# A new order of loads and steps at the start of a two-layer backbone kernel

## The chip, the cores and the metric

The kernel runs on one core of one Trainium2 chip. The core has the engines PE (matrix products, with its weight loads shown apart as PEld), DVE (vector), ACT (scalar functions), POOL (general) and SP (here it only issues transfers). Each engine takes its own instructions in order and waits on semaphores for the others. The metric is the device time in microseconds of one execution.

## The reference, cut to what matters

The model has two layers over 256 latent tokens `x` and 256 context tokens `h` of width 1024. The first sub-layer is a SwiGLU of both token sets, each normalised and modulated with its own scale and shift:

```
m  = silu(c) @ ada_w[0] + ada_b[0];   mc = silu(c_ctx) @ ada_w[0] + ada_b[0]
u  = rmsnorm(x, norm_g[0, 0]) * (1 + m[1]) + m[0]       # the same for h with mc
x += 0.5 * m[2] * ((silu(u @ wg) * (u @ wu)) @ wd)      # wg, wu: 1024 x 2816; wd: 2816 x 1024
```

Then come a state-space mixer, a second SwiGLU, and a second layer with a pooling mixer between two SwiGLUs, each sub-layer with its own scale, shift and gate out of `ada_w`. Only the start of the first sub-layer is changed.

## The kernel before

Activations lie with channels on the partitions: eight tiles of 128 channels by 512 tokens (256 of context, 256 latent). A weight block of 128 output channels is one load of 128x1024 floats (512 KB). Each product of float32 values is made of three matmuls on parts rounded to fp32r: ACT rounds the weight (`hi`, L203), DVE takes the rest (`lo`, L208), the operand is split likewise (`uh`, `ul`), and `mm3` (L216 to L218) adds high x high, low x high, high x low.

The start of the kernel, called the stage below, makes the operands of the first products and the first six weight blocks' products. It is written as a string, `WAVE`: each letter is one step, and the n-th occurrence of a letter is the step's n-th index. The order of the letters is the order in which the instructions are handed to the framework, which fixes each engine's queue at build time and may let an instruction that it holds ready pass earlier ones that wait.

- `X` loads one block of 128 tokens as two halves of 512 channels (tokens on the partitions), `v` (DVE) and `q` (ACT) square and sum the halves, `z` (DVE) adds the two sums, `r` (POOL) takes the power -0.5, and `s` (DVE, eight of them) scales a half by it.
- `A` loads two tiles of the scale and shift weights for one block of 128 channels (`adan`, ten buffers), `c` multiplies them with silu(c) on PE (two groups of instructions, one for each tile), `R` copies the row out (ACT), `e` turns it into columns on PE, `f` adds the constants (DVE).
- `t` turns the scaled tokens of one channel block on PE into the one bank `xc`, `m` scales and shifts out of that bank (DVE), `u` rounds (ACT), `n` takes the rest (DVE). Then one of eight operands is there.
- `L` loads a weight block (six, in six buffers), `h` rounds it (ACT), `k` takes the rest (DVE).
- `b` and `B` spread silu(c) over the partitions for later use.
- `p` is one cell: the product of one weight block with one operand, three matmuls of 512 columns. There are 6 x 8 cells, and the string `CELLS` gives their order ("21" is block 2 with operand 1).

Behind the stage the products of the other weight blocks follow, of two blocks and 16 cells for each index `f`. ACT's `sg` (L336) takes the first block of a pair when its eight cells are done. Among these products the weights for the other scales, shifts and gates are loaded and multiplied on DVE (`adaw`, L142 and L145); their buffers take the place of those of `adan`, so their loads wait for the stage's last `m`.

Of the kernel before, what the change touches and what calls it, by code (L numbers as in the profile page):

```python
# [15 lines left out]
P = 128  # L16
# [29 lines left out]

WAVE = (
    "AAXXXXLbAbBAcBALcRvqAezbRrfAqvebLBfzqvrqvzBzrshsrscALLLsktRcmeRefutfchnmpRckuetRenphfpf"  # L50
    "cmcRkuethpnpfhpmphkpRpukeppnpfpskppspspsptpmputpmpnutpmpnutpmpnuppnpppppppppppppppppppp"
)
CELLS = "00 10 01 11 20 02 12 21 22 30 31 32 03 13 23 33 40 41 42 43 50 51 52 04 14 05 15 24 06 07 16 17 25 26 27 34 35 36 37 44 45 46 47 53 54 55 56 57"

POOL_O = (1, 3)
POOL_Z = (1, 3)
# [10 lines left out]
def tile_hybrid_backbone(  # L67
# [20 lines left out]
    v, sc, pe, gp = nc.vector, nc.scalar, nc.tensor, nc.gpsimd  # L88
# [13 lines left out]
    def bank(nm, tag):  # L102
        if tag == "c":
            turn[0] ^= 1
            tag = f"c{turn[0]}"
        return ps.tile([P, 512], F32, tag=f"ps{tag}", name=nm, bufs=PSUM_BANKS[tag])

    def tmp(nm, tag, n=512):
        return tp.tile([P, 512], F32, tag=f"t{tag}", name=nm)[:, 0:n]
# [12 lines left out]
    XH = [xres.tile([P, 2 * S], F32, name=f"x{d}") for d in range(KD)]  # L122
    X = [t[:, LAT] for t in XH]
    cs = const.tile([P, 4 * P], F32, name="cs")
    ident, tri = cs[:, 0:P], [cs[:, P : 2 * P], cs[:, 2 * P : 3 * P]]
# [49 lines left out]
    def scale_cols(l, i, sub, nm):  # L175

        s = mcol(l, i, 3 * sub + 1, nm + "s")
        o = const.tile([P, KD], F32, name=nm + "a")
        g0 = C_NG + (3 * l + sub) * KD
        v.scalar_tensor_tensor(o, s, 1.0, pk[:, g0 : g0 + KD], op0=ALU.add, op1=ALU.mult)  # L180
        return o
# [100 lines left out]
    def utiles(T):  # L282
        uh = [upool[0].tile([P, T], F32R, name=f"uh{d}", tag=f"uh{d}") for d in range(KD)]
        ul = [upool[0].tile([P, T], F32R, name=f"ul{d}", tag=f"ul{d}") for d in range(KD)]
        return uh, ul
# [92 lines left out]
    u = utiles(2 * S)  # L378
    with ExitStack() as st:
# [22 lines left out]
        ads, prs, xcs, mts, raws, his, ws, outs = [], [], [], [], [], [], [], {}  # L402
# [31 lines left out]
        def w_b(j):  # L434
# [3 lines left out]
                pe.transpose(o[:, i * P : (i + 1) * P], cT[:, k % KD, k // KD : k // KD + 1].to_broadcast([P, P]), ident)  # L438
            bcs.append(o)

        def w_B(j):
            sc.activation(cb2[j // 2][:, (j % 2) * 512 : (j % 2 + 1) * 512], bcs[j], AF.Copy)

# [33 lines left out]
            )  # L477
            v.tensor_scalar(b00[:, d, :], pr[:, 2:4], col(C_AB, d), None, op0=ALU.add)

        def w_t(d):  # L480

            assert at["s"] >= 4 + d // 4 * 4
            x = bank("xc", "c1")
            for j in range(4):
                c = slice(d % 4 * P, (d % 4 + 1) * P)
                pe.transpose(x[:, j * P : (j + 1) * P], XH[2 * j + d // 4][:, c], ident)
            xcs.append(x)

        def w_m(d):
            assert len(xcs) > d and at["f"] > d  # L490
            x = xcs[d]
            t = tmp("mt", "a")
            for tok, i in ((ONE, 1), (LAT, 0)):
                a, b = a00[:, d, i : i + 1], b00[:, d, i : i + 1]
                v.tensor_scalar(t[:, tok], x[:, tok], a, b, op0=ALU.mult, op1=ALU.add)
            mts.append(t)
# [16 lines left out]
        def w_p(i):  # L513
            b, k = (int(c) for c in CELLS.split()[i])
            assert at["k"] > b and at["n"] > k
            if k == 0:
                outs[b] = bank("gu", "a" if b < 4 else "b")
            prod(outs[b], ws[b], k, u, ALL)

        steps = {  # L520
            "X": w_X, "v": w_v, "q": w_q, "z": w_z, "r": w_r, "s": w_s, "b": w_b, "B": w_B, "A": w_A, "c": w_c, "R": w_R,
            "e": w_e, "f": w_f, "t": w_t, "m": w_m, "u": w_u, "n": w_n, "L": w_L, "h": w_h, "k": w_k, "p": w_p,
        }
        at = dict.fromkeys(steps, 0)
        for what in WAVE:
            steps[what](at[what])
            at[what] += 1
        assert sorted(CELLS.split()) == [f"{b}{k}" for b in range(6) for k in range(KD)]
        assert [at[i] for i in "bBXvqzrsAcReftmunLhkp"] == [4, 4] + [4] * 5 + [8] * 10 + [6] * 3 + [48]
        st2.close()  # L530
        later = deque((XH[d], hxT[d * P : (d + 1) * P, :]) for d in range(KD))
        later.append((cs[:, P : 3 * P], tris))
# [57 lines left out]
    with ExitStack() as st:  # L590
# [4 lines left out]
        u = utiles(2 * S)  # L595
        a = [vecs[0].a, scale_cols(0, 1, 1, "a011")]
        b = [vecs[0].b, mcol(0, 1, 3, "b011")]
# [266 lines left out]
        o = ready.pop(24)  # L864
# [7 lines left out]
        def t64(nm, tag):  # L872
            return tmp(nm, tag, 256).rearrange("p (j c) -> p j c", c=64)

        dtk = scp.tile([P, 4, 64], F32, name="dtk")
        e, w, nr, ln = t64("dte", "a"), t64("dtw", "a"), t64("dtn", "b"), t64("dtl", "b")
# [29 lines left out]
        for d in range(2):  # L906
            c = slice(32 * d, 32 * d + 32)
# [17 lines left out]
        for j, d, k in ((0, 0, 1), (1, 1, 0)):  # L925
            c = slice(32 * d, 32 * d + 32)
# [4 lines left out]
        for d in range(2):  # L931
            c = slice(32 * d, 32 * d + 32)
# [14 lines left out]
        at = dict.fromkeys(steps, 0)  # L947
# [113 lines left out]
    for g in range(NG):  # L1061
        o = bank("pq", "b")[:, 0:S]
        channels(o, g, lambda t, k: t[k][:, S : S + 1].to_broadcast([P, P]))
        t = XH[g][:, ONE]
# [10 lines left out]
    for g in range(NG):  # L1075
        qh, ql = [], []
        for j in range(2):
            q = tmp("q", "b", S)
            v.scalar_tensor_tensor(q, pq[g, j], rtok[:, j : j + 1], bq[g], op0=ALU.mult, op1=ALU.add)
            a = work.tile([P, S], F32R, tag="qh", name="qh", bufs=3)  # L1080
            sc.activation(a, q, AF.Copy)
            b = work.tile([P, S], F32R, tag="ql", name="ql", bufs=3)
# [3 lines left out]
        for dd in range(2):  # L1086
            d = 2 * g + dd
            o = bank("pp", "c")[:, 0:S]
            pmh, pml = pm[g // 2]
            for j in range(2):  # L1090
                c = slice((2 * (g % 2) + j) * S, (2 * (g % 2) + j + 1) * S)
                dc = slice(dd * P, (dd + 1) * P)
                mm3(o, qh[j][:, dc], ql[j][:, dc], pmh[:, c], pml[:, c], j == 0, j == 1)
            t = tmp("pt", "d", S)
# [8 lines left out]
    for d2 in range(KD // 2):  # L1103
        o = tp.tile([P, 2, S], F32, tag="t" + "abcd"[d2], name="ot")
        for q in range(2):
            d = 2 * d2 + q
# [4 lines left out]
def _layout(inputs):  # L1111
    import numpy as np

    a = {k: np.asarray(x) for k, x in inputs.items()}
    f = np.float32

    def cols(x):
        return x.reshape(-1, P).T

    def tiles(w, nk):  # L1120

        n = w.shape[1] // P
        return w.reshape(nk, P, n, P).transpose(2, 1, 0, 3).reshape(n, P, nk * P)

    pack = np.concatenate(
        [
            cols(a["norm_g"]), cols(a["final_g"]), cols(a["ada_b"]),
            a["ssd_conv_w"][0].reshape(5, 24, P).transpose(2, 1, 0).reshape(P, 120),
            cols(a["ssd_conv_b"]), cols(a["pool_b"]), cols(a["pool_scale"]),
            np.concatenate([np.zeros(64, f), a["ssd_dt_bias"].reshape(64)])[:, None],  # L1130
            np.broadcast_to(a["ssd_a_log"].reshape(1, 64), (P, 64)),
            np.broadcast_to(a["ssd_d"].reshape(1, 32), (P, 32)),
            np.stack([a["c"].reshape(D), a["c_ctx"].reshape(D)]).reshape(2, KD, P).transpose(2, 1, 0).reshape(P, 16),
        ],
        axis=1,
    )
    assert pack.shape[1] == C_END
    i = np.arange(P)
    tris = np.concatenate(
        [i[:, None] <= i[None, :], i[:, None] >= i[None, :]], axis=1  # L1140
    ).astype(f)
    pm = np.zeros((NG, S, S))
    rows, width = S // 64, 64
    for g, w in enumerate((2, 4, 8, 16)):
        def box(n):
            p = np.arange(n)
            hi, lo = np.minimum(p + w - w // 2, n), np.maximum(p - w // 2, 0)
            return ((p[None, :] >= lo[:, None]) & (p[None, :] < hi[:, None])) / (hi - lo)[:, None]

        pm[g] = np.kron(box(rows), box(width)) - np.eye(S)  # L1150

    pmat = pm.transpose(0, 2, 1).reshape(2, 2, 2, P, S).transpose(0, 3, 1, 2, 4).reshape(2, P, 4 * S).astype(f)
    w_in = a["ssd_w_in"][0]
    wgu = np.stack(
        [
            np.stack([np.stack([tiles(a[n][l, s], KD) for n in ("ffn_w_gate", "ffn_w_up")]) for s in range(2)])
            for l in range(2)
        ]
    )
    wd = np.stack([np.stack([tiles(a["ffn_w_down"][l, s], NF) for s in range(2)]) for l in range(2)])  # L1160
    win = np.concatenate([tiles(w_in[:, 2048:5120], KD), tiles(w_in[:, 5056:5184], KD)])
    wz = w_in[:, :2048].reshape(4, 2, P, 4, 512).transpose(3, 0, 2, 1, 4).reshape(4, 4, P, 1024)
    wout = a["ssd_w_out"][0].reshape(4, 4, P, 4, 2, P).transpose(0, 3, 2, 4, 1, 5).reshape(4, 4, P, 1024)
    pw = a["pool_w"][0].reshape(2, 2, 2, P, 256).transpose(0, 3, 1, 2, 4).reshape(2, P, 1024)

    adan = np.stack([tiles(a["ada_w"][0][:, i * D : (i + 1) * D], KD).reshape(KD, P, KD, P) for i in (1, 0)], axis=3)
    adan = adan.reshape(KD, P, 2 * D)
    ada = np.stack([a["ada_w"][l].T.reshape(72, P, D) for l in range(2)])
    return {
        "hx": np.concatenate([a["ctx"][0], a["x"][0]]),  # L1170
        "hxT": np.concatenate([a["ctx"][0].T, a["x"][0].T], axis=1),
                "pack": pack, "idn": np.eye(P, dtype=f), "tris": tris, "pmat": pmat, "gnorm": a["ssd_norm_g"].reshape(1, 2048),
        "ada": ada, "adan": adan, "wgu": wgu, "wd": wd, "win": win, "wz": wz,
        "wout": wout, "poolw": pw,
    }
# [20 lines left out]
```

## Time and profile before

| | |
|---|---|
| timed runs | 1315.9 us median of 3 (1314.4 to 1316.13) |
| the profiled execution | 1308.84 us, of which the span of all instructions 1307.1 us |
| busy share of the span | PE 95%, PEld 85%, DVE 74%, ACT 46%, POOL 12% |
| first of 40 slices (0 to 32.7 us) | PE 50%, DVE 30%, granted clock of PE 0.7, transfers 90% or more |
| the slices after it | PE mostly 90% or more |
| mean granted clock of PE | 0.984 |

An engine's busy time counts its instructions, without semaphore waits and without issuing transfers. Matmuls are pipelined, so the length of one is longer than its distance to the next. The granted clock is given as a part of 2.4 GHz.

### The profile page before, as it was taken

Reading aid. Unit: us, or ns where it says so; the run is one execution under the profiler, and the core shown is the slowest. Engines: PE = TensorE matmul, PEld = TensorE weight load, DVE = VectorE, ACT = ScalarE, POOL = GpSimd, SP = SyncE. Lnnn points to the kernel's source line nnn. Section 1 sums busy time; section 2 is a strip of 40 time slices with the busy share of each in tenths; the row PEclk is TensorE's granted clock in tenths of the full one; section 3 lists DMA queues with packets and bytes.
Section 4 is the critical chain, followed back from the end, with each engine's and each line's share of the span. In section 5 each row is a group of like instructions: output and inputs, shape, how many; then the busy total and the mean of one; then the engine's idle time right before and its main releaser. Section 6 shows DMA issues by size and latency. Waiting matters only on the chain.

```text
span 1307.1 us, 21106 instructions
## 1 busy us (share of the span) xinstructions
PE 1248.1 (95%) x8262; PEld 1110.3 (85%) x8262; DVE 972.6 (74%) x1545; ACT 596.7 (46%) x1023; POOL 157.9 (12%) x112
## 2 busy tenths in 40 slices
PE   5999999999999979999988999999999999999997
PEld 2688888888888757787776999999999999999997
DVE  3599988763367879988997998766978566965553
ACT  3342222222244766555453654544545446744441
POOL 1000000000003242434263300000200000200000
PEclk7999999999999989999999999999999999999999
DMA  9588888962223513434343599767689665375661
GB/s 351 185 312 278 270 314 310 312 226 86 76 93 105 176 52 123 160 115 146 134 148 118 194 326 323 263 207 243 240 311 314 184 207 189 106 240 194 181 184 33
DMA packets 74995, 262.45 MB, mean 201 GB/s; under 512 B 8272, under 2 KB 10768, under 8 KB 73872
## 3 DMA queue, kind: packets, MB, share of 16 engines
q1 hardware_dynamic: 74896, 261.11, 59.1%
q8 instruction: 65, 1.06, 0.3%
q14 instruction: 34, 0.28, 0.1%
HBM read 259.96 MB, written 1.11 MB: 200 GB/s over the span
## 4 chain that ended last, share of the span: by engine, by line
PE 76%; DVE 9%; DMA 5%; ACT 4%; issue 3%; POOL 3%; SPq 0%; POOLq 0%; DVEq 0%; ACTq 0%
PE gu L218 14%; PE gu L216 14%; PE gu L217 14%; PE dn L216 7%; PE dn L218 7%; PE dn L217 7%; DMA adaw<-in_ada_dram 4%; DVE lo L208 2%; DVE ca L630 1%; POOL em L743 1%; PE ip L218 1%; PE ip L217 1%; PE ip L216 1%; PE py L803 1%; PE po L807 1%
## 5 line engine op out<-in xcount | busy, mean ns | idle before, releaser
L208 DVE TENSOR_TENSOR lo<-raw,hi 128x1024 fp32r<-128x1024 f32 (+1 forms) x317 | 393.3, 1244 | 145.9 <-ACT hi L203 145.3
L203 ACT ACTIVATE hi<-raw 128x1024 fp32r<-128x1024 f32 (+1 forms) x333 | 342.0, 1037 | 299.9 <-PE dn L218 125.8
L216 PE MATMUL gu<-vh,hi 128*128 128x256 f32 (+1 forms) x1056 | 293.3, 278 | 4.5 <-DVE sg L1002 2.6
L218 PE MATMUL gu<-vl,hi 128*128 128x256 f32 (+1 forms) x1056 | 292.5, 277 | 0.2 <-DVE vl L991 0.2
L217 PE MATMUL gu<-vh,lo 128*128 128x256 f32 (+1 forms) x1056 | 292.6, 277 | 0.0
L145 DVE SCALAR_TENSOR_TENSOR junk<-adaw,cb 128x1024 bf16<-128x1024 f32 x152 | 183.9, 1222 | 43.9 <-DMA adaw<-in_ada_dram 43.2
L216 PE MATMUL dn<-hh,hi 128*128 128x256 f32 (+1 forms) x704 | 214.2, 304 | 0.0
L217 PE MATMUL dn<-hh,lo 128*128 128x256 f32 (+1 forms) x704 | 214.2, 304 | 0.0
L218 PE MATMUL dn<-hl,hi 128*128 128x256 f32 (+1 forms) x704 | 214.2, 304 | 0.0
L216 PEld LDWEIGHTS gu<-vh,hi 128*128 128x128 f32 x1056 | 198.7, 188 | 5.2 <-DVE sg L1002 2.8
L218 PEld LDWEIGHTS gu<-vl,hi 128*128 128x128 f32 x1056 | 198.4, 188 | 0.5 <-DVE vl L991 0.4
L217 PEld LDWEIGHTS gu<-vh,lo 128*128 128x128 f32 x1056 | 198.6, 188 | 0.0
L218 PEld LDWEIGHTS dn<-hl,hi 128*128 128x128 f32 x704 | 132.1, 188 | 6.9
L217 PEld LDWEIGHTS dn<-hh,lo 128*128 128x128 f32 x704 | 132.1, 188 | 6.9
L216 PE MATMUL gu<-uh,hi 128*128 128x512 f32 x352 | 138.0, 392 | 0.0
L216 PEld LDWEIGHTS dn<-hh,hi 128*128 128x128 f32 x704 | 132.1, 188 | 6.8
L218 PE MATMUL gu<-ul,hi 128*128 128x512 f32 x352 | 137.9, 392 | 0.0
L217 PE MATMUL gu<-uh,lo 128*128 128x512 f32 x352 | 137.4, 390 | 0.0
L257 POOL TENSOR_TENSOR rs<-ms,mhalf 128x2 f32<-128x2 f32 (+1 forms) x6 | 5.4, 906 | 934.4 <-DVE ms L255 934.4
L307 ACT ACTIVATE hh<-hf 128x256 fp32r<-128x256 f32 (+1 forms) x88 | 40.9, 465 | 91.5 <-DVE hf L338 90.0
L336 ACT ACTIVATE sg<-gu 128x256 f32<-128x256 f32 (+1 forms) x79 | 34.7, 439 | 98.2 <-PE gu L218 98.2
L218 PEld LDWEIGHTS gu<-ul,hi 128*128 128x128 f32 x352 | 66.2, 188 | 15.2 <-issue 0.8
(264 smaller groups left out, 1883.6 us busy)
## 6 DMA issues: line engine op xcount, KB each, us to landing
raw<-in_wgu_dram SPq DMA_DIRECT2D x176, 512.0 KB, 4.6
adaw<-in_ada_dram SPq DMA_DIRECT2D x128, 512.0 KB, 5.0
raw<-in_wd_dram SPq DMA_DIRECT2D x64, 512.0 KB, 3.7
raw<-in_win_dram SPq DMA_DIRECT2D x25, 512.0 KB, 3.4
raw<-in_wd_dram SPq DMA_DIRECT2D x32, 384.0 KB, 3.6
adan<-in_adan_dram SPq DMA_DIRECT2D x16, 512.0 KB, 8.4
raw<-in_wz_dram SPq DMA_DIRECT2D x16, 512.0 KB, 3.7
em<-acd SPq DMA_DIRECT2D x8, 1024.0 KB, 4.8
```

Of the source, the lines that this page charges most:

```text
L145: v.scalar_tensor_tensor(junk, w, 1.0, cb2[i], op0=ALU.mult, op1=ALU.mult, accum_out=M[l][:, t, i : i + 1])
L203: sc.activation(hi[:, 0:n], r[:, 0:n], AF.Copy)
L208: (sub or v).tensor_tensor(lo[:, 0:n], r[:, 0:n], f32(hi[:, 0:n]), op=ALU.subtract)
L216: pe.matmul(out, wh, xh, start=start, stop=False)
L217: pe.matmul(out, wl, xh, start=False, stop=False)
L218: pe.matmul(out, wh, xl, start=False, stop=stop)
L307: sc.activation(a, h, AF.Copy)
L336: sc.activation(sg, pg, AF.Silu)
L630: v.scalar_tensor_tensor(avw[:, :, lo:hi], ov[:, :, lo + off : hi + off], hw[:, 5 * t + k : 5 * t + k + 1], avw[:, :, lo:hi], op0=ALU.mult ...
L743: gp.tensor_tensor(EM[0][:, :, j, :], EM[0][:, :, j, :], EM[1][:, :, j, :], op=ALU.add)
L803: pe.matmul(py[:, hc], EM[0][:, h, j, :], xl[:, hc], start=True, stop=True)
L807: pe.matmul(po, CT[:, j * P : (j + 1) * P], hin[d][0 if j == d else 1], start=True, stop=True)
```

## The change

The string `WAVE` is written anew: the four token blocks are loaded ahead of the `A` tiles, the six weight loads stand between the `A` loads, and the steps that use them are listed in another order. `CELLS` is listed anew, too: the first three weight blocks take all eight operands, then the other three follow one block at a time. The step `t` becomes one turn of 128x128, 32 of them, where it was four turns in one step. A new step `W` turns the unit matrix four times into a bank that nobody reads; 17 of them are listed. A last hunk only mends the indentation of a line.

```diff
 WAVE = (
-    "AAXXXXLbAbBAcBALcRvqAezbRrfAqvebLBfzqvrqvzBzrshsrscALLLsktRcmeRefutfchnmpRckuetRenphfpf"
-    "cmcRkuethpnpfhpmphkpRpukeppnpfpskppspspsptpmputpmpnutpmpnutpmpnuppnpppppppppppppppppppp"
+    "XXXXAAAbLbBAbBLvbqAWWWWBzrvqLsBtzWWWWrqvstzqWWWvrzsrtWstsscALssWRecALfmWReutttftcALnWmRhetttftWWukcmpRnutttt"
+    "ehnpfpkcmpRhetttftpukpcmphnttttpukpRpnecfhmpRpkuettttfcnphmpRkpuettnttpfpmppupnpppppppppppppppppppppppppppp"
 )
-CELLS = "00 10 01 11 20 02 12 21 22 30 31 32 03 13 23 33 40 41 42 43 50 51 52 04 14 05 15 24 06 07 16 17 25 26 27 34 35 36 37 44 45 46 47 53 54 55 56 57"
+CELLS = "00 01 02 10 11 12 20 21 03 13 04 14 22 05 15 23 06 16 24 25 26 07 17 27 30 31 32 33 34 35 36 37 40 41 42 43 44 45 46 47 50 51 52 53 54 55 56 57"
...
+        def w_W(j):
+            o = bank("warm", "b")
+            for i in range(4):
+                pe.transpose(o[:, i * P : (i + 1) * P], ident, ident)
...
-        def w_t(d):
-
-            assert at["s"] >= 4 + d // 4 * 4
-            x = bank("xc", "c1")
-            for j in range(4):
-                c = slice(d % 4 * P, (d % 4 + 1) * P)
-                pe.transpose(x[:, j * P : (j + 1) * P], XH[2 * j + d // 4][:, c], ident)
-            xcs.append(x)
+        def w_t(i):
+
+            d, j = i // 4, i % 4
+            assert at["s"] > d // 4 * 4 + j
+            if j == 0:
+                xcs.append(bank("xc", "c1"))
+            c = slice(d % 4 * P, (d % 4 + 1) * P)
+            pe.transpose(xcs[d][:, j * P : (j + 1) * P], XH[2 * j + d // 4][:, c], ident)
 
         def w_m(d):
-            assert len(xcs) > d and at["f"] > d
+            assert at["t"] >= 4 * d + 4 and at["f"] > d
```

## Rows read from the trace of the kernel before

**Rows 1.** Busy time in stretches: PE, PEld, DVE, ACT, POOL; clock, DMA share, GB/s

```profile
7.00:13.00 6.00, 3.38 (x38) 1.28 (x39) 0.70 (x2) 1.26 (x3) 0.00 (x0) 1.00 1.02 390
14.00:26.00 12.00, 3.92 (x17) 2.05 (x17) 8.55 (x25) 4.08 (x10) 2.99 (x4) 0.50 1.04 409
26.90:30.60 3.70, 3.70 (x17) 1.76 (x15) 1.47 (x3) 0.90 (x2) 0.00 (x0) 0.50 1.03 411
33.00:39.00 6.00, 3.79 (x33) 2.19 (x33) 3.61 (x10) 2.60 (x5) 0.00 (x0) 1.00 1.03 410
40.00:78.00 38.00, 38.00 (x210) 28.68 (x208) 26.03 (x45) 15.18 (x22) 0.00 (x0) 1.00 0.52 189
80.00:100.00 20.00, 20.00 (x89) 16.53 (x89) 20.00 (x32) 5.22 (x8) 0.00 (x0) 1.00 0.89 309
```

**Rows 2.** Groups by line and form up to 79 us: busy, mean ns, idle before

```profile
L216 PE MATMUL gu<-uh,hi 128*128 128x512 f32 x50 | 20.5, 412 | 0.0
...
L203 ACT ACTIVATE hi<-raw 128x1024 fp32r<-128x1024 f32 x12 | 12.4, 1053 | 3.4 <-PE gu L218 2.9 <-DMA raw<-in_wgu_dram 0.5
L208 DVE TENSOR_TENSOR lo<-raw,hi 128x1024 fp32r<-128x1024 f32 x10 | 12.1, 1219 | 0.0
...
L495 DVE TENSOR_SCALAR mt<-xc,a,b 128x256 f32<-128x256 f32 x16 | 7.9, 539 | 1.4 <-PE xc L486 1.2
...
L502 DVE TENSOR_TENSOR ul<-mt,uh 128x512 fp32r<-128x512 f32 x8 | 5.5, 688 | 3.9 <-ACT uh L499 3.9
...
L464 ACT ACTIVATE row<-pr 128x256 f32<-128x256 f32 x8 | 3.1, 385 | 18.2 <-PE pr L459 10.3 <-PE pr L470 7.5 <-DVE b L478 0.4
...
L474 DVE TENSOR_SCALAR a<-pr,sb,pk 128x2 f32<-128x2 f32 x8 | 2.2, 277 | 12.4 <-PE pr L470 11.5 <-ACT row L464 0.8
...
L423 DVE TENSOR_SCALAR ss<-ss 128x1 f32<-128x1 f32 x4 | 0.8, 206 | 0.0
```

**Rows 3.** ACT in order of time: start, length, instruction, idle before

```profile
83.49 0.60 ACT L336 ACTIVATE sg<-gu 128x512 f32<-128x512 f32 x1 [3.29 <-PE gu L218]
...
94.37 0.60 ACT L336 ACTIVATE sg<-gu 128x512 f32<-128x512 f32 x1 [3.82 <-PE gu L218]
```

**Rows 4.** Chain of waits in order of time, first 30 us

```profile
15.77 0.95 POOL rs L427
...
22.77 0.50 DVE x L432
23.31 0.49 PE xc L486
...
25.41 1.01 PE pr L459 x8
```

**Rows 5.** PE in order of time, first 56 us

```profile
3.83 3.04 PE L438 MATMUL bc<-cs,cT 128*128 128x128 f32 x13 [3.83 <-ACT cT L391]
7.35 0.64 PE L459 MATMUL pr<-adan,cT 128*32 128x256 f32 x8 [0.49 <-DMA adan<-in_adan_dram]
...
12.65 0.61 PE L470 MATMUL pr<-sel,row 128*128 128x2 f32 x4 [0.50 <-ACT row L464]
...
26.91 0.78 PE L216 MATMUL gu<-uh,hi 128*128 128x512 f32 x1
...
55.33 0.60 PE L486 MATMUL xc<-cs,x 128*128 128x128 f32 x4
55.69 0.48 PE L217 MATMUL gu<-uh,lo 128*128 128x512 f32 x1
```

**Rows 6.** ACT in order of time, about 17 us

```profile
16.98 0.63 ACT L419 ACTIVATE ja<-x 128x512 f32<-128x512 f32 x1 [0.62 <-DMA x<-in_hx_dram]
17.52 0.18 ACT L419 ACTIVATION_READ_ACCUMULATOR ja<-x 128x1 f32 x1
18.20 1.06 ACT L203 ACTIVATE hi<-raw 128x1024 fp32r<-128x1024 f32 x1 [0.50 <-DMA raw<-in_wgu_dram]
```

**Rows 7.** DVE in order of time, behind the stage

```profile
84.63 1.22 DVE L208 TENSOR_TENSOR lo<-raw,hi 128x1024 fp32r<-128x1024 f32 x1
```

More of the change, by code (lines that the diff above doesn't have):

```diff
@@ L521, in tile_hybrid_backbone @@
             "X": w_X, "v": w_v, "q": w_q, "z": w_z, "r": w_r, "s": w_s, "b": w_b, "B": w_B, "A": w_A, "c": w_c, "R": w_R,
-            "e": w_e, "f": w_f, "t": w_t, "m": w_m, "u": w_u, "n": w_n, "L": w_L, "h": w_h, "k": w_k, "p": w_p,
+            "e": w_e, "f": w_f, "t": w_t, "m": w_m, "u": w_u, "n": w_n, "L": w_L, "h": w_h, "k": w_k, "p": w_p, "W": w_W,
         }
@@ L528, in tile_hybrid_backbone @@
         assert sorted(CELLS.split()) == [f"{b}{k}" for b in range(6) for k in range(KD)]
-        assert [at[i] for i in "bBXvqzrsAcReftmunLhkp"] == [4, 4] + [4] * 5 + [8] * 10 + [6] * 3 + [48]
+        assert [at[i] for i in "bBXvqzrsAcRefmunLhktp"] == [4, 4] + [4] * 5 + [8] * 9 + [6] * 3 + [32, 48]
         st2.close()
@@ L1171, in _layout @@
         "hxT": np.concatenate([a["ctx"][0].T, a["x"][0].T], axis=1),
-                "pack": pack, "idn": np.eye(P, dtype=f), "tris": tris, "pmat": pmat, "gnorm": a["ssd_norm_g"].reshape(1, 2048),
+        "pack": pack, "idn": np.eye(P, dtype=f), "tris": tris, "pmat": pmat, "gnorm": a["ssd_norm_g"].reshape(1, 2048),
         "ada": ada, "adan": adan, "wgu": wgu, "wd": wd, "win": win, "wz": wz,
```

## Prediction

> **What bounds the kernel now.** I read the page first (its shares are in the table above): TensorE (PE) is the bound nearly everywhere, except in the first of the forty slices. The change touches only this first stage, so I went on with windows of it. From 14 to 26 us the transfers run at 409 GB/s, share 1.0, and PE works 3.9 us of 12 at a granted clock of 0.50; from 33 to 39 us it works 3.8 of 6; from 40 to 78 us it has no gap and the transfers are at half [rows 1]. So the stage has two halves: first the loads and the chain behind them starve PE, then PE alone sets the pace until the first products end.
>
> When do they end? Up to 79 us each of the three product lines has run 50 times; the stage has 48 cells, so two cells of the next product are in it [rows 2]. ACT's sg steps at 83.49 and 94.37 show 10.88 us for a product pair of 16 cells, 48 matmuls: 0.227 us a matmul, 0.68 a cell. The 48 cells end at 83.49 - 8 x 0.68 = 78.05 us, since the first of these sg waits for the first eight cells behind the stage; both ways give 78.0 [rows 3]. **E = 78.0 is the number that the change must lower.** Behind it PE runs on without a gap, so what E gains reaches the end, unless something behind it is late (last rival).
>
> The chain of waits shows what is late before it: the powers and scalings of the four token rows, from 15.77 to 23.27, and the fourth turn at 23.31 [rows 4]. The first cell starts at 26.91 [rows 5].
>
> **The loads, listed anew.** 512 KB (an adan tile, a pair of token halves, a weight) take 0.524 MB / 408 GB/s = 1.285 us, one after another. Landings seen: the first adan tile at 7.35, the last token pair, eighth in line, at 16.98, the first weight at 18.20 [rows 5, 6]. Continuing by 1.285, the 26th and last lands at 40.0, where the transfers do slacken. The change keeps the bytes and permutes the places: token pairs 7.4, 9.0, 10.3, 11.5; A0 complete at 14.3, A1 17.0, A2 19.5, weight L0 20.8, A3 23.3, L1 24.6, A4 27.2, L2 28.5, A5 31, L3 32.3, A6 34.9, L4 36.1, A7 38.7, L5 40.0. A5 to A7 reuse the buffers of A0 to A2, and SP waits there for their c steps; c2 can run from 19.5 on and A7's place is the one that ends at 38.7, so I cost this wait at nothing (if c2 came over 10 us late, A7 and L5 behind it would be late next).
>
> **First cell.** The last token row lands at 11.5. Its q takes 0.63 + 0.19, z 0.2, r 0.95, s 0.50, turn 0.49 [rows 2, 4, 6]: 14.5, and with its queueing on DVE 15. It is 23.8 now, 6.8 us after landing, because v of a row stands on DVE behind f, which waits for PE and ACT. A0 lands at 14.3: c 0.64, R 0.39, e 0.61, two f of 0.28, two m of 0.54, u 0.63 (as q, same engine and size), n 0.69 [rows 2, 5, 6] give 18.9 for the first operand. L0 lands at 20.8, hi takes 1.05 and lo 1.22 [rows 2]: 23.1. So the first cell can run at S = 23.1, set by its weight, 3.8 us before now.
>
> **PE's work from there.** Before, first cell to last: 78.0 - 26.9 = 51.1 us. In it PE is idle 6.0 - 3.8 = 2.2 us from 33 to 39, and from 26.9 to 30.6 its granted clock is 0.50 (1.2 of 2.4 GHz), which costs half of 3.7 us, 1.85 [rows 1]. Without both it is 47.0; one half of c2 (0.6) then lies ahead of S: 46.5 us.
>
> Is there always work? Ready at 23.1: cells 00 and 01, c3, e and turns; 02 from 24.5; L1, split at 26.9, gives three cells, the fourth operand (near 28) two, L2 (30.8) four, the fifth operand (near 32) three, L3 (34.6) five, each operand also 1.15 us of c, 0.6 of e, 0.4 of turns. Up to 40 that is some 25 us of work for 17 us of PE. So it is never short by much, if the queues serve it. DVE has per operand two f, two m and n, 2.3 us by their rows, and 1.2 per weight: some 20 us from 23 to 43, its whole time (a little less, since the rows overlap). I bound the stalls by 0 (supply as above) and by the 2.2 us of now, and take 2.2, the row of the same stage, since DVE has no room. For the clock the bounds are 0 and 1.85; I take 0: between 15 and 23 us c, e and turns fill PE to over half, as from 7 to 13 us before (3.4 of 6, granted 1.00) and unlike 14 to 26 (3.9 of 12, granted 0.50) [rows 1].
>
> E = 23.1 + 46.5 + 2.2 = 71.8; gain 6.2 us.
>
> **The unit-matrix turns (W).** 17 x 4 = 68 turns of 128x128. Four take 0.36 us at full clock (55.33 to the next at 55.69); 13 take 3.04 at the start, where the clock is low [rows 5]. That is 0.09 and 0.23 each, in all 6.1 to 15.9 us of PE. They wait for nothing and nobody reads them. PE has 16.2 us between the end of the b turns (6.9) and S, of which c0 to c2, e0 to e2 and three sets of turns need 7; 9 are free, so I cost the 68 at nothing there; without this cover they cost their time (rival). Cutting t into single turns moves nothing by itself: the turn at 23.31 already runs singly, when its row is scaled [rows 4]. The built order need not be the listed one: the fourth b is listed behind the first c, and its first turn is among the 13 that run before it [rows 5]. So W may run earlier than listed, which is harmless.
>
> What turns do to the clock: after 13 turns and nothing else on PE, the c group at 7.35 takes 0.64 us, against 1.0 for one in the chain at low clock [rows 4, 5]. So turns did raise it. The Trainium skill ("TensorE: Matmul & The Clock Gate", Part 4: PE-mode transpose) says that turns don't count as PE being busy for the clock; this trace disagrees. By that rule the first cells would run at 1.2 GHz as now and the sum be 1.85 us more.
>
> **Rivals.**
> - *Clean* (0.20): no stalls, E 69.6, or 68.4 if the first matmul of a cell goes as soon as hi is there (21.9). Gain 8.4 to 9.6: 1306.3 to 1307.5. For it: the supply. Against: DVE is full.
> - *Clock stays down* (0.13): granted 0.50 before S, then half speed for 3.7 us as now: E 73.7, gain 4.3, 1311.6. For it: 0.50 from 14 to 30 us now. The skill's rule just named would make it so.
> - *The queues stall again* (0.12): the list, as built, puts m or k on DVE behind something that waits, as v now. With the first cell at 26.9 again and 4.05 us lost as now E is 77.5; a gain of 0 to 2.6, 1313.3 to 1315.9.
> - *Turns in the way* (0.10), the slower one: PE has no spare time behind S, so each turn built behind it, or ahead of a c or e that the chain waits for, lengthens the path. All 68 at 0.09 add 6.1: no change. At 0.23 they add 15.9: E 87.7, 1325.6. It turns slower by over 0.2% once 8.8 us are on the path: 38 of the 68 at low clock. Against: at low clock PE is by that very fact waiting a lot, and turns fill waits.
> - *Absorbed later* (0.03): DVE is busy 20 of 20 us from 80 to 100 [rows 1]. Against: the lo at 84.63, the fifth one behind the stage's own six, is needed by PE at 78.0 + 4 x 5.44 = 99.8, 14 us after its end [rows 7]. A lead of 6 us fits in that, and the ada loads that fill DVE wait for the last m, so they start earlier too.
>
> **The numbers.** The profiled execution took 1308.84 us with a span of 1307.1; the timed runs have a median of 1315.9, 0.5% more. I take the gain as absolute: 1308.84 - 6.2 = 1302.6 for a like execution, and 1315.9 - 6.2 = 1309.7 as the forecast, chance 0.42, its own range 1307.5 to 1311.6. About 0.2% (2.6 us) is what a measurement here tells from no change. Faster: forecast, clean, clock: 0.75. Within: stalls again and absorbed: 0.15. Slower: 0.10. The range runs from 1305.0 (clean, and DVE a little ahead) to 1317.0 (stalls again, or some turns in the way), and leaves out 0.2.
>
> **What would show it.** Scalings of the token rows over by 15 us; first cell at 22 to 24; granted clock near 1.0 from 23 to 31; the last adan group on PE near 39, and the ada loads soon after 42; sg of the fourth pair at 77 instead of 83.5. It is wrong if the first cell stays at 26 us, if PE shows gaps over 3 us in all after it, if unit-matrix turns stand among the cells, or if sg comes earlier and the end does not.

## The result, and the profile after

The changed kernel takes 1308.57 us (median of 20 runs, 1304.66 to 1314.24), the kernel before, on the same chip and in turn with it, 1315.49 (20 runs, 1309.19 to 1328.12). The ratio is 0.9949 with a 95% interval of 0.9931 to 0.9966: faster by 6.7 us (1315 x 0.0051), 4.5 to 9.1. The forecast was 1309.7 with a range of 1305.0 to 1317.0. The time is right; one large step on the way to it is not.

The profiled execution took 1309.67 us (span 1307.9), longer than the one of before, 1308.84 (span 1307.1). So spans say nothing here, and I compare the stage. Its windows in the changed kernel, as in [rows 1] (PE, PEld, DVE, ACT, POOL; clock, DMA share, GB/s):

```profile
7.00:13.00 6.00, 5.49 (x47) 5.25 (x46) 3.69 (x12) 3.55 (x10) 2.79 (x3) 1.00 0.98 378
14.00:26.00 12.00, 9.84 (x92) 5.81 (x91) 4.89 (x15) 2.50 (x6) 0.72 (x1) 1.00 1.02 408
26.90:30.60 3.70, 3.65 (x26) 1.88 (x27) 2.86 (x5) 0.95 (x3) 0.00 (x0) 1.00 1.02 407
33.00:39.00 6.00, 5.91 (x43) 3.85 (x47) 3.60 (x7) 2.43 (x4) 0.00 (x0) 1.00 1.03 406
40.00:78.00 38.00, 38.00 (x202) 28.73 (x201) 27.30 (x46) 15.16 (x21) 0.00 (x0) 1.00 0.54 198
80.00:100.00 20.00, 20.00 (x90) 16.57 (x89) 20.00 (x32) 5.71 (x7) 0.00 (x0) 1.00 0.92 336
```

From 14 to 26 us PE works 9.84 us in place of 3.92, and the granted clock is 1.00 in place of 0.50; 33 to 39 has hardly a gap. The transfers are as busy as before. ACT in order of time:

```profile
24.76 0.38 ACT L470 ACTIVATE row<-pr 128x256 f32<-128x256 f32 x1 [1.20 <-PE pr L465]
25.28 0.63 ACT L505 ACTIVATE uh<-mt 128x512 fp32r<-128x512 f32 x1
25.81 1.04 ACT L204 ACTIVATE hi<-raw 128x1024 fp32r<-128x1024 f32 x1
...
79.10 0.60 ACT L337 ACTIVATE sg<-gu 128x512 f32<-128x512 f32 x1 [1.70 <-PE gu L219]
89.98 0.60 ACT L337 ACTIVATE sg<-gu 128x512 f32<-128x512 f32 x1 [2.60 <-PE gu L219]
```

E, the end of the 48 first cells, is read as in the prediction, but from the fifth sg, because in one experiment the fourth stands late on ACT itself: start less 10.88 less 5.44. Before: 94.37 - 16.32 = 78.05, the same as by the fourth [rows 3]. After: 89.98 - 16.32 = **73.66**, 4.4 us earlier (forecast 6.2). And PE from the last turn of the first channel block to the first cell, and its last wait in the stage:

```profile
15.50 0.33 PE L493 MATMUL xc<-cs,x 128*128 128x128 f32 x1 [0.53 <-DVE x L433]
...
16.32 0.98 PE L445 MATMUL warm<-cs 128*128 128x128 f32 x7
17.24 0.64 PE L465 MATMUL pr<-adan,cT 128*32 128x256 f32 x8
17.81 0.65 PE L445 MATMUL warm<-cs 128*128 128x128 f32 x4
18.38 0.61 PE L476 MATMUL pr<-sel,row 128*128 128x2 f32 x4
18.85 0.74 PE L445 MATMUL warm<-cs 128*128 128x128 f32 x5
...
20.09 0.65 PE L445 MATMUL warm<-cs 128*128 128x128 f32 x4
20.68 0.64 PE L465 MATMUL pr<-adan,cT 128*32 128x256 f32 x8
22.39 0.61 PE L476 MATMUL pr<-sel,row 128*128 128x2 f32 x4 [1.08 <-ACT row L470]
...
26.91 0.50 PE L217 MATMUL gu<-uh,hi 128*128 128x512 f32 x1 [0.61 <-ACT hi L204]
...
33.09 0.30 PE L493 MATMUL xc<-cs,x 128*128 128x128 f32 x1 [0.89 <-DVE mt L501]
```

The token rows are over nearly as early as forecast (last turn 15.50, forecast 15). But **the first cell is at 26.91, to the hundredth where it was** [rows 5], not at 23.1. It waits for hi, and hi at 25.81 stands on ACT behind the third R and the second u. The weight itself was there well before: L0's load was issued at 11.23, and the weight loads of the stage land 9.5 to 10.8 us after their issue, so it landed by 22.0. Ahead of the cell on PE, 20 unit-matrix turns (7, 4, 5, 4) stand among the `c` and `e` of the first two channel blocks. (Each of the eight operands is one channel block; the expectations below sometimes say token row for it.) What `f` waits for is on DVE:

```profile
21.46 0.28 DVE L480 TENSOR_SCALAR a<-pr,sb,pk 128x2 f32<-128x2 f32 x1 [5.61 <-PE pr L465]
```

Its own e ended at 18.99; it waits for the `c` of the next channel block, which ends at 21.3 in the same bank `pr`.

So 4.4 us were won behind a first cell that is no earlier. Theory after this reading: the turns hold the clock (1.85 of it), less idle time and work done ahead of the cell make the rest. Rivals: the clock came from the token rows alone; the first cell was the bound after all, and an earlier weight would give the missing 2 us.

### The profile page after: what moved, and what is told of

Read it like the earlier page. It is cut to its first block, busy times and chain, and to the rows that moved or that the text cites. A ratio compares the mean times of both kernels' runs of the same rounds, so it can differ in the third digit from the quotient of the medians.

```text
span 1307.9 us, 21250 instructions
## 1 busy us (share of the span) xinstructions
PE 1258.4 (96%) x8330; PEld 1122.9 (86%) x8330; DVE 973.0 (74%) x1545; ACT 597.0 (46%) x1023; POOL 160.4 (12%) x112
## 4 chain that ended last, share of the span: by engine, by line
PE 81%; DVE 7%; ACT 4%; POOL 3%; issue 3%; DMA 2%; SPq 0%; POOLq 0%; DVEq 0%; ACTq 0%
PE gu L219 15%; PE gu L218 15%; PE gu L217 15%; PE dn L219 8%; PE dn L217 8%; PE dn L218 8%; DVE lo L209 1%; DVE ca L636 1%; POOL em L749 1%; PE ip L219 1%; PE ip L218 1%; PE ip L217 1%; DMA em<-acd 1%; PE py L809 1%; ACT hi L204 1%
## 5 line engine op out<-in xcount | busy, mean ns | idle before, releaser
L217 PEld LDWEIGHTS gu<-uh,hi 128*128 128x128 f32 x352 | 66.1, 188 | 15.6 <-issue 1.2
```

Of the source, the lines that this page charges most:

```text
L217: pe.matmul(out, wh, xh, start=start, stop=False)
```

## The experiments

Each ratio is of 12 runs (the changed kernel's of 20, that of two_banks_l0 of 11, without the one of 1328.28 us), in turn with runs of the kernel before; every E, first cell and granted clock is that of one profiled execution.

| kernel | first cell | clock 14 to 26 | clock 23 to 27 | E | ratio to before |
|---|---|---|---|---|---|
| before | 26.91 | 0.50 | 0.50 | 78.05 | |
| before_again | 27.13 | 0.50 | 0.50 | 79.02 | |
| after | 26.91 | 1.00 | 1.00 | 73.66 | 0.9949 (0.9931 to 0.9966) |
| after_again | 26.68 | 1.00 | 1.00 | 73.34 | |
| t_joined | 26.50 | 1.00 | 1.00 | 73.17 | 0.9976 (0.9952 to 1.0000) |
| no_w | 28.08 | 0.50 | 0.50 | 75.66 | 0.9978 (0.9954 to 1.0001) |
| half_w | 25.07 | 0.77 | 0.50 | 74.01 | 0.9954 (0.9923 to 0.9985) |
| before_w | 29.25 | 0.88 | 0.51 | 80.44 | 1.0014 (0.9988 to 1.0041) |
| x_first | 25.42 | 0.84 | 0.50 | 76.06 | 0.9960 (0.9933 to 0.9988) |
| x_first_w | 25.72 | 0.91 | 0.60 | 74.56 | 0.9992 (0.9967 to 1.0016) |
| two_banks | 26.36 | 1.00 | 1.00 | 75.39 | 0.9976 (0.9943 to 1.0009) |
| l0_early | 23.78 | 1.00 | 1.00 | 73.46 | 0.9963 (0.9940 to 0.9987) |
| l0_earlier | 24.25 | 1.00 | 1.00 | 72.04 | 0.9972 (0.9946 to 0.9998) |
| two_banks_l0 | 22.30 | 0.86 | 0.79 | 75.68 | 0.9976 (0.9940 to 1.0011) |

In x_first the clock column does not agree with the lengths of the matmuls. It reads 1.00 up to 22 us, but the first `c` there are as long as at a granted 0.50 (1.08 us for eight; half_w has the same 1.08 at 25.78 with 0.50, the changed kernel 0.64 with 1.00):

```profile
14.36 1.08 PE L459 MATMUL pr<-adan,cT 128*32 128x256 f32 x8
...
15.81 2.79 PE L459 MATMUL pr<-adan,cT 128*32 128x256 f32 x24
```

Before the column's first change it can be too high, as it is in the first 7 us of every profile here (1.00, with turns of 0.23 us). In no_w, half_w and the changed kernel the two agree from 13 us on.

**The same kernels again (after_again, before_again).** No edit.

> The changed kernel itself, once more, nothing edited: how far the end of the 48 first cells (the end of the fourth pair's gating step on ACT less 5.44 us) and the later stages vary from one execution to the next. If the first stage is set by its order, the end comes again at 73.4 to 73.9, the first cell at 26.9 and the granted clock is 1.00 in 14 to 31 us. If the long PE step from 900 to 1060 us (0.117 us a matmul against 0.1127) was of that one execution, it is absent here or stands elsewhere; if it belongs to the changed kernel, it stands there again.

> The kernel before itself, once more, nothing edited, to see how far the end of the 48 first cells and the clock of the first 30 us come again in another execution. If the stage is set by its order, the end comes again at 77.7 to 78.4 us, the first cell at 26.7 to 27.1, with a granted clock of 0.50 from 14 to 30.6 us.

The changed kernel's stage comes again within 0.3 us, and most of that is when the tokens come: from the last turn of the first channel block (15.50 and 15.27, in t_joined 15.10) to E it is 58.16, 58.07 and 58.07 us. That of before comes 1.0 later. Its first cell is 0.2 later, and its clock fell once more: from 33 to 39 us it was granted 0.86, 1.00 in [rows 1]. The windows of before_again:

```profile
14.00:26.00 12.00, 3.70 (x15) 2.04 (x17) 8.56 (x25) 4.31 (x10) 2.99 (x4) 0.50 1.00 364
...
33.00:39.00 6.00, 4.29 (x31) 2.44 (x31) 3.43 (x10) 2.43 (x5) 0.00 (x0) 0.86 1.02 408
```

From these few executions I take it that two E less than about 1 us apart are not told apart where the clock is low, and 0.5 where it is full.

**The turns taken away (no_w).** The changed list without its 17 W:

```diff
-    "XXXXAAAbLbBAbBLvbqAWWWWBzrvqLsBtzWWWWrqvstzqWWWvrzsrtWstsscALssWRecALfmWReutttftcALnWmRhetttftWWukcmpRnutttt"
+    "XXXXAAAbLbBAbBLvbqABzrvqLsBtzrqvstzqvrzsrtstsscALssRecALfmReutttftcALnmRhetttftukcmpRnutttt"
```

> The changed kernel without its 17 W steps, all else listed as it is. E is the end of the 48 first cells (sg of the fourth pair less 5.44 us): 78.0 before, 73.7 in the changed kernel. Theory, the turns hold the clock: granted clock falls to 0.50 before 20 us and comes back near 30, the first cells run at half speed, E 75.5 to 77, the end 2 to 3 us later than with W. Rival, turns do not count for the clock and only stand in the queue: granted clock the same with and without them, the second half of c0 goes at about 15 us instead of 17.2, E 72.5 to 73.7, the end 0 to 1 us earlier.

E 75.66, 2.0 us later than with W, as the theory had it. Windows of no_w:

```profile
14.00:26.00 12.00, 9.96 (x61) 4.48 (x60) 4.59 (x12) 1.40 (x3) 0.71 (x1) 0.50 1.03 411
...
27.00:31.00 4.00, 4.00 (x22) 2.56 (x22) 2.94 (x6) 1.50 (x2) 0.00 (x0) 0.57 1.03 410
```

PE is as busy here as with W (9.96 against 9.84 us of 12), at 0.50 in place of 1.00: without the turns the same `c` and `e` take longer (16 matmuls of `c` 1.93 us here, 1.07 at full clock) and fill the same time. So PE busy for over half of a stretch did not raise the clock, though the prediction argued with just that. Nor did the clock come from the token rows alone, since they are first here, too. The 2.0 us rest on the profiles: the intervals of the two ratios overlap.

**Half of the turns (half_w).** About every second W left out of the changed list: 9 W, 36 turns, in place of 17 and 68.

```diff
-    "XXXXAAAbLbBAbBLvbqAWWWWBzrvqLsBtzWWWWrqvstzqWWWvrzsrtWstsscALssWRecALfmWReutttftcALnWmRhetttftWWukcmpRnutttt"
+    "XXXXAAAbLbBAbBLvbqAWWBzrvqLsBtzWWrqvstzqWWvrzsrtstsscALssWRecALfmReutttftcALnWmRhetttftWukcmpRnutttt"
```

> The changed kernel with 9 W in place of 17 (36 unit-matrix turns in place of 68): as built, the turns among the c products of the first two token rows are gone and those of the first 13 us are left. If few turns hold the clock as well as many, the granted clock is 1.00 from 14 to 31 us and the end of the cells comes at 72.8 to 73.7, as in the changed kernel or a little earlier, since no turn stands ahead of a product. If the turns between 13 and 21 us are what holds it, the clock falls to 0.50 in 20 to 30 us and the end comes at 75 to 76, as without any W.

The clock falls as the second case said, but E, at 74.01, is only just past the range of the first. Stretches of 1 us of half_w, then its PE in order of time:

```profile
19.00:20.00 1.00, 0.46 (x4) 0.46 (x4) 0.96 (x3) 0.38 (x1) 0.00 (x0) 1.00 1.01 406
20.00:21.00 1.00, 0.96 (x10) 0.57 (x10) 0.45 (x3) 0.63 (x1) 0.00 (x0) 0.73 1.05 418
21.00:22.00 1.00, 1.00 (x13) 0.54 (x16) 0.92 (x2) 0.00 (x0) 0.00 (x0) 0.50 1.05 418
```

```profile
16.86 0.61 PE L476 MATMUL pr<-sel,row 128*128 128x2 f32 x4 [0.49 <-ACT row L470]
17.39 1.07 PE L465 MATMUL pr<-adan,cT 128*32 128x256 f32 x16
19.54 0.61 PE L476 MATMUL pr<-sel,row 128*128 128x2 f32 x4 [1.08 <-ACT row L470]
...
25.07 0.78 PE L217 MATMUL gu<-uh,hi 128*128 128x512 f32 x1
```

The second `e` is at 19.54 in place of 22.39: 2.85 us earlier. Of this, 0.46 was there before (the last turn of the first channel block is at 15.04 in place of 15.50). The other 2.4 stand against the 20 turns that are gone from ahead of it, which took 0.98 + 0.65 + 0.74 + 0.65 = 3.0 in the changed kernel. So those turns do stand in the way, for most of their time. Leaving them out is paid for with the clock, which here is at half from about 20.5 to 30.7 (granted 0.73 in 20:21, 0.65 in 30:31). The two nearly cancel: E is 0.35 later than the changed kernel's, 0.8 with the earlier tokens counted.

**The turns alone (before_w).** The kernel before with 17 W spread over the first 60 letters of its list.

```diff
-    "AAXXXXLbAbBAcBALcRvqAezbRrfAqvebLBfzqvrqvzBzrshsrscALLLsktRcmeRefutfchnmpRckuetRenphfpf"
+    "AAXXXXLbAbBAcBALcRvWqAezWbRrWfWAqvWebLBfWzWqvWrWqvWzWBzWrWsWhsWrWsWcALLLsktRcmeRefutfchnmpRckue"
```

> The kernel before, with 17 W steps added in its own list and nothing else changed. Theory, the turns hold the clock: granted clock 1.00 from 14 to 31 us instead of 0.50, E 75 to 76.2 instead of 78.0, the end 2 to 3 us earlier than before. Rival, turns do not count: granted clock 0.50 from 14 to 30 as before, E 78.0 to 79, the end unchanged or later.

Both theories missed. The clock is held while the turns last; but the build runs a turn as soon as nothing else is ready, and they were used up before 20 us, with the token rows still to come. Windows of before_w:

```profile
14.00:26.00 12.00, 8.15 (x64) 6.11 (x62) 7.62 (x24) 4.16 (x11) 3.00 (x4) 0.88 1.03 402
20.00:23.00 3.00, 0.49 (x3) 0.28 (x2) 2.31 (x7) 0.00 (x0) 0.55 (x1) 1.00 1.01 406
23.00:27.00 4.00, 1.67 (x10) 0.38 (x9) 3.16 (x7) 0.00 (x0) 0.55 (x1) 0.51 1.02 412
```

PE is mostly idle from 20 on, the clock falls at 23, and the first cell is at 29.25. The last token row's turn is 1.2 us later than before, too (24.52 against 23.31); why, I did not test. W without the earlier token rows is worth nothing here.

**The token rows alone (x_first).** Two letters moved in the kernel before: the first two pairs of adan tiles behind the token rows.

```diff
-    "AAXXXXLbAbBAcBALcRvqAezbRrfAqvebLBfzqvrqvzBzrshsrscALLLsktRcmeRefutfchnmpRckuetRenphfpf"
+    "XXXXAALbAbBAcBALcRvqAezbRrfAqvebLBfzqvrqvzBzrshsrscALLLsktRcmeRefutfchnmpRckuetRenphfpf"
```

> The kernel before with only the four token loads moved ahead of the first two pairs of adan loads. Theory, this order alone brings the scaled rows early but the first operand then waits for its adan tiles and the clock is low: fourth turn at 15 to 17 us instead of 23.3, granted clock 0.50 from about 13, E 76 to 78, the end 0 to 2 us earlier. Rival, the order of the loads is nearly the whole gain: E 74.5 or less, the end 3.5 us or more earlier.

E 76.06, 2.0 earlier than before, at the early end of what was expected. The first cell is 1.5 earlier, at half clock. The expected 0.50 from 13 us on is not what came: by the lengths of the matmuls the clock was low up to about 18.6 us, high to 22 (the `e` at 19.10 takes 0.61, as at full clock), and low again for the first cell.

**Token rows and turns, old order of the rest (x_first_w).** The list of x_first with 17 W spread from its 22nd letter to the first cells (`...vqAWWWWezbRrfAqvebWWWWLBfzqvWWWrqvzBzrshsrWWsc...cmWWeReWWf...`).

> The kernel before with two parts of the change and without the third: the token rows' loads ahead of the adan weight's, and 17 W (68 unit-matrix turns) spread over the list up to the first cells; the order of the cells, of the other loads and of the steps is that of before. Token rows alone gave an end of the cells at 76.06, with a granted clock of 0.50 to 0.86 from 20 to 35 us. If the turns hold the clock up to the first cell, the time at half clock (some 2 to 3.5 us of PE's work) is won and the end comes at 73 to 74.5, level with the changed kernel: the list made anew is then worth nothing by itself. If the list made anew carries a part of its own, the end stays at 75 to 76.5, with idle time of PE in the first 12 us after the first cell.

E 74.56, just past the first case's range: 1.5 better than without W, 0.9 to 1.4 behind the three executions of the changed kernel's order (73.17 to 73.66). That difference is not the list alone, since the clock here fell to 0.60 in 23 to 27 us. Without W the new list gains less: no_w's 75.66 against x_first's 76.06. So the list made anew is worth 0.4 to 1.4 us, the smallest part, and hardly more than what E varies by. Its time (0.9992) came out worse than its E says; the interval just holds E's gain (1 - 3.5/1315 = 0.9973).

**Tokens turned all at once (t_joined).** In the changed list each group of four t stands together, behind the last scaling it needs.

```diff
-    "XXXXAAAbLbBAbBLvbqAWWWWBzrvqLsBtzWWWWrqvstzqWWWvrzsrtWstsscALssWRecALfmWReutttftcALnWmRhetttftWWukcmpRnutttt"
+    "XXXXAAAbLbBAbBLvbqAWWWWBzrvqLsBzWWWWrqvszqWWWvrzsrWsttttsscALssWRecALfmWReufttttcALnWmRhefttttWWukcmpRnutttt"
```

> The changed kernel with every token's four turns listed together, after the last of the scalings that they read, as in the kernel before (XXXXAAAb...r W s tttt ss and so on); the 17 W, the loads and the cells stay. As built, only the first token row's turns change place: the W come in one go of 48 turns ahead of them, and they follow one another near 15.5 us in place of 11.05, 11.77, 13.66 and 15.50. If turning tile by tile is worth something, the products c behind them are later and the end of the 48 cells comes at 74 to 74.5 us; if it is worth nothing, since the last of the four scalings sets the last turn either way, the end comes again at 73.3 to 73.7 us and the granted clock is 1.00 from 7 to 31 us.

E 73.17: turning tile by tile is worth nothing here, since the last scaling sets the last turn (15.10) either way.

**The weight earlier (l0_early, l0_earlier).** The first weight L0 is loaded ahead of the third pair of adan tiles, A2 (l0_early), or of the second, A1 (l0_earlier), and its `h` and `k` are listed early.

```diff
-    "XXXXAAAbLbBAbBLvbqAWWWWBzrvqLsBtzWWWWrqvstzqWWWvrzsrtWstsscALssWRecALfmWReutttftcALnWmRhetttftWWukcmpRnutttt"
+    "XXXXAALAbbBAbBLvbqAWWWWBzrvqLsBtzWWWWrqvstzqWWWvrzsrtWstsscALssWRehcALfmkWReutttftcALnWmRetttftWWucmpRnuttt"
...
+    "XXXXALAAbbBAbBLvbqAWWWWBzrvqLsBtzWWWWrqvstzqWWWvrzsrtWstsscALssWRehcALfmkWReutttftcALnWmRetttftWWucmpRnuttt"
```

> The changed kernel with the first weight L0 listed ahead of the third chunk of the adan weight, and with the splits h and k of the first weight listed ahead of the step e and the products of the second token row. Nothing else changes. Theory of the prediction (the first cell sets the stage): the weight's high part is ready near 20 to 21, the first cell comes at 23 to 24.5 instead of 26.9, PE fills its idle time of 3.2 us between 20 and 27 with cells, and the end of the 48 cells comes at 70 to 72.5 instead of 73.66. Rival (PE's work ahead of the cells is only moved behind the first one, since the later operands still wait for the adan weight): the first cell comes earlier, but the end stays at 73 to 74.5, with new idle time of PE of 1 us or more between 27 and 39.

> As the run before, with L0 ahead of the second chunk of the adan weight, so that this weight's first products (two of c) come one transfer, 1.3 to 2.6 us, later. Theory (first cell): it comes near 23.5, the end at 70.5 to 72.5, as in the run before or later by at most 1.3. Rival (the adan weight sets it): the two later chunks cost what they are late, so that the end is later than in the run before by 1 to 2.6 us, 74 to 76.

l0_early is the test of the step that failed, and it says that S was not the bound: the first cell is 3.1 us earlier, E 0.2. PE of l0_early:

```profile
23.78 0.49 PE L217 MATMUL gu<-uh,hi 128*128 128x512 f32 x1 [0.25 <-ACT uh L505]
24.21 0.64 PE L465 MATMUL pr<-adan,cT 128*32 128x256 f32 x8
24.78 0.49 PE L218 MATMUL gu<-uh,lo 128*128 128x512 f32 x1
...
25.66 0.64 PE L465 MATMUL pr<-adan,cT 128*32 128x256 f32 x8
```

The cell has taken the place of `c`, which follows later: work changed its order. PE's idle time from 14 to 80 us fell from 3.71 to 2.96 us, but E by 0.2 only, so most of what was filled came back as longer work: among the `c` the cell's three matmuls start 0.43 to 0.45 us before what follows them, where matmuls in a row start 0.23 apart. The rival's E came, but not its sign: from 27 to 40 us PE has no more idle time than in the changed kernel. In l0_earlier hi is done at 19.3; PE's idle time falls to 2.43, and E is 1.6 earlier, though the first cell is later than in l0_early (24.25). So the number is the first theory's and its cause is not. The rival, that late adan tiles cost what they are late, is wrong: it had 74 to 76.

What E does go with is PE's last long wait in the stage, for the `m` of the fourth operand, which frees the one bank `xc` for the turns of the fifth channel block. These turns start at 33.09 in the changed kernel (shown above), and in l0_early and l0_earlier at

```profile
32.77 0.41 PE L493 MATMUL xc<-cs,x 128*128 128x128 f32 x2 [0.86 <-DVE mt L501]
```

```profile
31.06 0.41 PE L493 MATMUL xc<-cs,x 128*128 128x128 f32 x2 [0.66 <-DVE mt L501]
```

In all nine profiles with the new order of the cells E comes 40.4 to 41.0 us after this turn (no_w 35.12, half_w 33.44, two_banks 35.00), wherever the first cell was. In the changed kernel this operand is late at least in part because the second half of its `c` (29.52) stands on PE behind matmuls that wait for the first weight's lo (done at 28.56); in l0_earlier lo is early and that half runs at 27.55. This is read from the profiles; no run moved this wait alone.

**Two banks for pr (two_banks, two_banks_l0).** `c` and `e` of every second channel block write another bank, so that `f` no longer waits for the next `c`; the second kernel also has the list of l0_earlier.

```diff
-        prt = bank("pr", "c0")
+        prt = [bank("pr", "c0"), bank("pr2", "b")]
...
-            pr = prt[:, d % 2 * S : (d % 2 + 1) * S]
+            pr = prt[d % 2][:, 0:S]
```

> The changed kernel with the c products of even and odd channel blocks in two banks (the second one of tag b) instead of two halves of one bank. Theory, f of block 0 waits for c of block 1 because both are in one bank: f at about 19 us instead of 21.5, first operand 2 us earlier, less idle time of PE between 20 and 35 (2.0 us or less, 3.2 in the changed kernel), E 71.5 to 73. Rival, the first cell hangs on the first weight's hi on ACT (25.8 us) and PE on the supply behind it: f earlier, E 73.4 to 74.

> The changed kernel with two edits together: the first weight L0 listed ahead of the second chunk of the adan weight (its split listed early too), and two banks in turn for the products pr, so that the step f of one token row no longer waits for the c of the next. The list as built then puts 18 of the unit-matrix turns around the first cell. Each edit alone left something open: the early weight gave an end of the cells of 72.04 with the operand as the last wait, the two banks gave an operand 3 us earlier with the clock down to 0.74 to 0.83 for 8 us and an end of 75.39. Theory (operand and weight bound the first cell together, and the clock holds because the cells follow the turns at once): first cell at 20.5 to 22, granted clock 1.00 through 31, the end at 69.5 to 71.5. Rival (the later chunks of the adan weight set the pace from 22 on): the first cell comes early, but PE has 1.5 us or more of idle time between 22 and 35 and the end stays at 72 to 73.5. Second rival (the clock falls again): 0.7 to 0.85 somewhere between 20 and 35 and the end at 73.5 to 76.

The shared bank is shown: with two, DVE's f of two_banks waits for its own `e` alone and is 3.1 us earlier (2.7 counted from the last turn of the first channel block, 15.06 there).

```profile
18.32 0.28 DVE L480 TENSOR_SCALAR a<-pr,sb,pk 128x2 f32<-128x2 f32 x1 [2.93 <-PE pr L476]
```

But E gets worse than the changed kernel's, by 1.7 and 2.0, against both expectations of two_banks. The first cell of two_banks does wait for hi on ACT, as its rival had it. And the clock falls in both kernels; why it falls, and how much of the loss is the clock's and how much the order's, no run shows. Windows of two_banks, then of two_banks_l0:

```profile
23.00:27.00 4.00, 3.28 (x25) 1.69 (x21) 2.31 (x6) 1.96 (x3) 0.00 (x0) 1.00 1.03 411
27.00:31.00 4.00, 3.28 (x20) 1.79 (x24) 2.31 (x4) 0.63 (x1) 0.00 (x0) 0.74 1.02 409
31.00:35.00 4.00, 2.88 (x17) 1.61 (x10) 1.55 (x5) 1.44 (x3) 0.00 (x0) 0.83 1.03 411
```

```profile
20.00:23.00 3.00, 2.69 (x18) 1.92 (x19) 1.89 (x3) 0.63 (x1) 0.00 (x0) 0.71 1.04 412
23.00:27.00 4.00, 4.00 (x32) 2.06 (x31) 1.02 (x4) 0.39 (x1) 0.00 (x0) 0.79 1.02 407
```

In two_banks_l0 the operand and the weight are both early and the first cell is at 22.30, the earliest of all; still the second rival holds (E 73.5 to 76). PE of two_banks_l0:

```profile
20.31 0.63 PE L493 MATMUL xc<-cs,x 128*128 128x128 f32 x4 [1.70 <-DVE mt L501]
...
21.53 1.12 PE L445 MATMUL warm<-cs 128*128 128x128 f32 x4
22.30 0.78 PE L217 MATMUL gu<-uh,hi 128*128 128x512 f32 x1
22.87 0.84 PE L445 MATMUL warm<-cs 128*128 128x128 f32 x3
23.64 1.08 PE L465 MATMUL pr<-adan,cT 128*32 128x256 f32 x8
```

After a wait of 1.70 us turns and cell run at low clock (four turns 1.12 in place of 0.65, the cell's first matmul 0.78 in place of 0.50), and the turns now stand around the first cell. Some of the loss is theirs, some the clock's; this run does not part them. Its profiled execution took 1328.28 us (median 1313.91), so only its first stage is used.

No version beats the changed kernel by more than can be measured. l0_earlier has the lowest E, by 1.1 to 1.6 us, a tenth of a per cent.

## Why the prediction was right

- **E is the number, and it reaches the end: right.** Over the eleven versions with a ratio E lies 3.1 us below the 78.05 of before on average, and the times 3.5 us (1315 times the mean of 1 - ratio). For the change itself E fell by 4.4 in the two profiles. With both executions of before (78.5) and the three with the changed kernel's order (73.4) it is 5.1, against 6.7 (4.5 to 9.1) by the clock on the chip. *Absorbed later* did not happen. This holds on average; version by version E and time differ by up to 3.3 us (x_first gained 2.0 in E and 5.3 in time, x_first_w 3.5 and 1.1), about what the intervals allow.
- **Loads and token rows: right.** The last `q` starts at 11.96 and the last turn of the first channel block at 15.50; forecast 11.5 and 15.
- **First cell: wrong, the step that failed.** The step was "set by its weight", S = 23.1; that the first cell stays at 26 us was my own sign of being wrong, and it came. The place of L0 was not the limit: hi was queued on ACT behind `R` and `u`, which wait for the operand chain, and this chain was late, because `f` waits for the next `c` in the bank that they share (2.5 us) and because 20 turns stand ahead of `c` and `e` (3.0, of which 1.4 lie inside that wait). I had added up the chain's durations for one channel block, 18.9, without what its engines do for the next. And S should not have carried the sum: l0_early moved it by 3.1 us for 0.2 of E. E goes with the fourth operand's `m` instead, the last long wait behind which PE runs on.
- **Work behind S: the right terms, other sizes.** From 26.91 to 73.66 are 46.75 us. Some 0.95 of it is idle (0.89 at 33 us and bits), where I took 2.2, since DVE did have room: 3.60 us of 6 from 33 to 39. The rest is 45.8 in place of 46.5; I put this down to more `c`, `e` and turns ahead of the cell. So: S 3.8 later, idle 1.25 less, work 0.7 less: 71.8 + 3.8 - 1.25 - 0.7 = 73.65. That two smaller errors took back half of the large one is luck. So is some of the hit in time: the stage's 4.4 to 5.1 us alone would give 1310.8 to 1311.5, and the measured gain has an interval of 4.5 to 9.1.
- **Clock: right, with a wrong reason beside a right one.** It was 1.00 from 14 to 31 us, and no_w puts the turns' share at 2.0 us of E (the term was 1.85). That c, e and turns fill PE was no reason: no_w is as full, at 0.50. E came out at the very 73.7 that I gave to *Clock stays down*, and its cause is none of that rival's; only the clock column tells them apart. The rule of the Trainium skill that stood against the change ("TensorE: Matmul & The Clock Gate", Part 4: PE-mode transpose) does not hold for these turns of float32: they are what differs between 0.50 in no_w and 1.00 in the changed kernel.
- **The turns at nothing: wrong for 20 of 68.** They were pulled forward, as I thought possible, and not all into free time: *Turns in the way* was at work, at some 2.4 us of the operand chain (half_w), but at full clock and ahead of the first cell, and the clock gave about as much back.
- **Ada loads soon after 42: wrong, with no effect that the times show.** They were issued from 57.71, since the last `c` came at 52.5, not 39, and the last `m`, for which they wait, ended at 57.5. The build had put ready cells ahead of the last `c`.

By parts, in E: token rows first 2.0 (x_first), the turns 1.5 on top of them (x_first_w) or 2.0 in the new list (no_w), the list made anew 0.4 to 1.4, turning tile by tile nothing. The turns need the token rows (before_w), but not the other way round. What stays open is how much of the last part is the order of the loads and how much that of the cells: the old order of the cells in the new list was not tried.

## What to carry to other kernels

Where a stage starves PE, count its idle time and its half-clock time in windows, and ask of a change which of them it fills; a single early milestone can move by 3 us and the end by 0.2. Look for the last wait behind which the bounding engine has no gap: what moves that wait moves the end. Before adding up a chain for one tile, follow each bank and each queue of it to the next tile's steps. Filler work for the clock has its price in the queue: have it end where the real work starts, and look in the built order at what it stands in front of.

## What the runs showed of the hardware that I had not expected

A busier PE can have the lower clock: from 20 to 23 us half_w is busy 2.86 us of 3 at a granted 0.58, the changed kernel 1.92 of 3 at 1.00. From 15 to 20 us half_w had run `c`, `e` and the last turn of the first channel block, the changed kernel the same with 20 unit-matrix turns between them.

PE's step also changes at a granted clock of 1.00. One stretch of the later products, PE without a gap in both, in the profile of the changed kernel and in that of after_again:

```profile
940.00:980.00 40.00, 40.00 (x342) 40.00 (x341) 32.37 (x52) 18.59 (x27) 0.00 (x0) 1.00 0.89 326
```

```profile
940.00:980.00 40.00, 40.00 (x356) 40.00 (x355) 32.88 (x52) 17.38 (x26) 0.00 (x0) 1.00 0.88 322
```

342 matmuls against 356 in the same 40 us: 0.117 us a step against 0.112, 1.6 us lost per 40. The first execution has this from 940 to 1060, after_again from 1200 to 1290 (766 matmuls against 797), the profile of half_w nowhere in what I counted (720 to 1290), and that is the shortest one (1301.15 us). The kernel before shows it in one execution, too (before_again, from 1140 on), and not in the other. So it belongs to the execution and not to the kernel. At 40 and 31 matmuls of 0.112 us it costs 3.5 to 4.5 us, under half of the spread from 1304.66 to 1314.24; what causes it no row shows.
